# Advancing the urgent and the ordinary queue of side work beside each weight tile, and moving where sums of activations are made

## The chip, the cores and the metric

One core of one Trainium2 chip runs the kernel. The metric is the device time of one execution in microseconds. TensorE (PE) multiplies, and PEld is its weight load; VectorE (DVE), ScalarE (ACT), GpSimd (POOL) and SyncE (SP) are the other engines.

## What is computed

One hybrid block on 256 tokens of width 4096, in fp32: an RMS norm, a wide projection, an mLSTM branch with eight heads, a sparse attention branch with sixteen heads in four groups, gates on both branches, an output projection with a residual, and a gated extra embedding at the end. Cut to what matters:

```python
h = _rmsnorm(x, norm_w[layer])
u = h @ w_in[layer]
(ml_q, ml_k, ml_v, ml_o, ml_z, ml_i, ml_f, ns_q, ..., ns_g, ns_z) = _split(u, IN_SPLITS)
...
hm = _rmsnorm(_mlstm(mq, mk, mv, log_i, log_f).astype(x.dtype), ml_head_norm_w[layer])
y_ml = hm.reshape(B, S, ML_WIDTH) * jax.nn.sigmoid(ml_o) * jax.nn.silu(ml_z)
y_ns = _nsa(...) * jax.nn.silu(ns_z)
x = x + jnp.concatenate([y_ml, y_ns], axis=-1) @ w_out[layer]
x = x + jax.nn.sigmoid(x @ ple_gate[layer]) * (p[layer] @ ple_proj[layer])
```

## The kernel before

The weights are streamed once through on-chip memory in tiles of 128 by 1024, and nearly all the time goes to products of such tiles with activations. A product in fp32 is made from three: ScalarE copies a tile `raw` to `whi` in a rounded format (L1308), VectorE subtracts to get the rest `wlo` (L1309), activations are split the same way into `sh` and `sl`, and TensorE adds up `whi` with `sh`, `whi` with `sl` and `wlo` with `sh`. The activations of one pass lie in eight chunks of 512 of the 4096 features, `sh[c]` and `sl[c]`, each of two halves; a half, 256 features, is called a kp (chunk c holds kps 2c and 2c+1).

The program is one list of units in a fixed order; a unit is one weight tile and its matmuls. The main loop splits the tile three units ahead (`LOOK = 3`), emits the unit's matmuls, calls its `post`, and then calls `step()`. There are first the "wide" groups, which make the projections `kc` to `mv3` (16 units each, L816 and L818), and then 14 "pair" groups: -6 to -1 make gates from the normed input (activations `x`), 0 to 3 the output projection (activations `y`), 4 to 7 the last gate (activations `r`). Groups from 4 on start with two `p` units for the extra embedding's own projection.

In a pair group the six kps of `MIXED` (3, 5, 7, 9, 11, 13) are computed with seven block products in place of eight. For that, sums of weight blocks are made on VectorE (`raw`, L1133 to L1137) and sums of activation blocks, which are called `cb`: VectorE forms four blocks `s` from additions and subtractions, ScalarE rounds them to `cb` (high part) and VectorE subtracts for the low part. I call that a mix of a kp. A mixed step is six units: two that open it (`a_units`), two of an ordinary kp (`c_unit`), two that close it (`c_units`). `PLANS` says which kps are mixed in which group: all six in most groups, 7, 9 and 11 in group -6, and 9, 11 and 13 in group 0. The first unit of a mixed step requires the flag of its mix, which `require` gets by calling `step()` until it is there.

Where the sums of activations are made differs by pass. For `x`, `t_xmix` makes all six in the order of `MIXED`; it is queued behind the last part of the mLSTM, when the last wide group ends. For `y` and `r`, `t_stat` transposes the finished activations chunk by chunk (L723), rounds them to `sh` (L734 to L744), subtracts for `sl` (L749 to L758), makes the blocks `s` of the chunk's mixed half from a copy (L762 to L764), and then `cb` (L768, L771). It is queued twice per pass: chunks 0 and 1 when group -1 (or 3) closes its last mixed step, chunks 2 to 7 at its end.

All work beside the matmuls is written as generators that stand in two queues: `urgent` (evacuation of finished accumulators: `t_evac`, `t_mv`, `t_gate_own`, `t_x1_oth`, `t_x1_own`, `t_out_own` and others) and `fifo` (all else, in order: attention, mLSTM, mixes, `t_stat`). `step()` takes one advance from the first queue that has one:

```python
def step():
    for queue in (urgent, fifo):
        while queue:
            try:
                next(queue[0])
                return True
```

`t_gate_own` adds a finished group's accumulators to `us` (L1037), applies the activation function on ScalarE (`u`, L1045) and multiplies on VectorE (`y`, L1051). The attention of one group of heads, `t_nq`, is a pipeline over eight units (head and half of the tokens) in which step i does the scores of unit i, their bias and maximum, the exponential, and for earlier units `coef` (reciprocal and multiplication, L511 and L512), `scale` (L516), `trans` (transposes, L523), `copy_pt` (copy of the transposed probabilities, L528) and `pv`.

Of the kernel before, what the change touches and what calls it, by code (L numbers as in the profile page):

```python
# [41 lines left out]


MIXED = (3, 5, 7, 9, 11, 13)


def _plan(head, mixed, between, tail):
# [25 lines left out]
def hymba_block(ctx: ExitStack, tc: tile.TileContext, a, out: bass.AP):  # L73
# [87 lines left out]
    fifo, urgent = deque(), deque()  # L161
    done = set()

    def step():
        for queue in (urgent, fifo):
            while queue:
                try:
                    next(queue[0])
                    return True
                except StopIteration:  # L170
                    queue.popleft()
        return False
# [242 lines left out]
    def t_nq(flag, g):  # L415
# [124 lines left out]
        def at(f, i):  # L540
            if 0 <= i < 8:
                f(i)

        for i in range(11):
            at(trans, i - 2)
            at(pv, i - 3)
            at(scores, i)
            at(copy_pt, i - 2)
            at(coef, i - 1)
            at(bias_max, i)  # L550
            at(scale, i - 1)
            at(expo, i)
            yield
        if g % 2 == 0:
# [121 lines left out]

    cb = {}

    def mixed_tiles(kp):
        if kp in (3, 5):  # L680
            t = wk.tile([128, 2, 4, 128], F32R, tag="qt", name="cb", bufs=2)
        elif kp == 7:
            t = wk.tile([128, 2, 4, 128], F32R, tag="sq", name="cb")
        elif kp == 13:
            return [wk.tile([128, 4, 128], F32R, tag="pt", name="cb", bufs=2) for _ in range(2)]
        else:
            if kp == 9:
                held["cb"] = wk.tile([128, 2, 2, 4, 128], F32R, tag="b", name="cb")
            t = held["cb"][:, int(kp == 11)]
        return t[:, 0], t[:, 1]  # L690

    def t_xmix():

        f = {}
        for i in range(len(MIXED) + 1):
            if i:
                nc.vector.tensor_sub(cb[MIXED[i - 1]][1], f[i - 1], cb[MIXED[i - 1]][0])
                done.add(f"x{MIXED[i - 1] // 2}m")
            if i == len(MIXED):
                return  # L700
            c, b = MIXED[i] // 2, 2 * (MIXED[i] % 2)
            v = f[i] = stile([128, 4, 128])
            nc.vector.tensor_add(v.rearrange("p a t -> p (a t)"), sh[c][:, b:b + 2].rearrange("p k t -> p (k t)"),
                                 sl[c][:, b:b + 2].rearrange("p k t -> p (k t)"))
            nc.vector.tensor_sub(v[:, 3:0:-2], v[:, 1::-1], v[:, 3:0:-2])
            nc.vector.tensor_sub(v[:, 0], v[:, 0], v[:, 3])
            nc.vector.tensor_sub(v[:, 2], v[:, 2], v[:, 0])
            yield
            cb[MIXED[i]] = mixed_tiles(MIXED[i])
            nc.scalar.activation(cb[MIXED[i]][0], v, AF.Copy)  # L710
            yield

    def t_stat(chunks, weighted, bset=1, pace=2):


        def chunk(c, col0, gate, flag):
# [10 lines left out]
            for half in range(2):  # L727
                p, hs = pp[half], slice(2 * half, 2 * half + 2)
                w = [hnw[:, col0 // 128 + 2 * half + i:col0 // 128 + 2 * half + i + 1] for i in range(2)] if scales else None
                if 2 * c + half in MIXED:  # L730
                    f[half] = stile([128, 4, 128])
                    if scales:
                        for i in range(2):
                            nc.scalar.activation(f[half][:, 2 * i:2 * i + 2].rearrange("p a t -> p (a t)"), p[:, i],  # L734
                                                 AF.Copy, scale=w[i])
                        nc.scalar.activation(sh[c][:, hs].rearrange("p k t -> p (k t)"),
                                             f[half].rearrange("p a t -> p (a t)"), AF.Copy)
                        continue
                    nc.scalar.activation(f[half].rearrange("p a t -> p (a t)"), p.rearrange("p a t -> p (a t)"), AF.Copy)
# [21 lines left out]
            for v in f.values():  # L761
                nc.vector.tensor_sub(v[:, 3:0:-2], v[:, 1::-1], v[:, 3:0:-2])  # L762
                nc.vector.tensor_sub(v[:, 0], v[:, 0], v[:, 3])
                nc.vector.tensor_sub(v[:, 2], v[:, 2], v[:, 0])  # L764
            yield
            for half, v in f.items():
                cb[2 * c + half] = mixed_tiles(2 * c + half)
# [3 lines left out]
                nc.vector.tensor_sub(cb[2 * c + half][1], v, cb[2 * c + half][0])  # L771
            done.add(flag + "m")

        under_way, waiting, pause = deque(), deque(chunks), 0
        while under_way or waiting:
            for _ in range(len(under_way)):
                g = under_way.popleft()
# [78 lines left out]
    def p1_post(name):  # L856
# [3 lines left out]
        def post(ps, flag):  # L860
# [13 lines left out]
            elif kind in ("mq", "mk"):  # L874
                evac(ps, flag)
                add(t_mqk(flag, int(kind == "mk"), i))
                if name == "mk0":
                    add(t_mlstm(0))
            elif kind == "mv":
                if i == 2:  # L880
                    require("nq3")
                urgent.append(t_mv(ps, flag, i))
                if i == 3:
                    add(t_mlstm(1), t_xmix())
        return post

    def small_group():
# [174 lines left out]
    def pair_group(g, w, stat):  # L1062
# [39 lines left out]
        def new_activations(g, chunks, b):  # L1102

            if g < 0:
                add(t_stat([(c, (c * 512 + 2048) % 4096, f"p1_{c}", f"y{c}") for c in chunks], range(16), b))
            else:
                add(t_stat([(c, c * 512, f"p2_{c}", f"r{c}") for c in chunks], (), b))

        def finish(kp):
            if g in (-1, 3):  # L1110
# [250 lines left out]
    for n in range(N):  # L1361
# [9 lines left out]
        if un["post"]:  # L1371
            un["post"]()
        if n >= 3:
            step()
    while step():
        pass

# [82 lines left out]
```

## Time and profile before

| what | value |
|---|---|
| median of 3 runs | 2183.65 us (2182.29 to 2184.06) |
| the profiled execution's own time | 2184.17 us |
| its span in the profile | 2182.4 us |
| mean granted clock of TensorE | 0.994 |
| TensorE matmul busy | 2149.3 us, 98% |
| TensorE weight load busy | 1761.2 us, 81% |
| VectorE busy | 1563.6 us, 72% |
| ScalarE busy | 1153.8 us, 53% |
| DMA, mean over the span | 193 GB/s |

The span runs from the first to the last instruction that the profile shows; the time of the execution has 1.8 us around it. Busy shares are averages over stages. Matmuls are pipelined and overlap in the trace: a row for one of 512 columns reads 0.39 us, while in a full stretch their starts are 0.22 to 0.23 us apart. A granted clock of 1.00 is 2.4 GHz, and 0.50 is 1.2 GHz.

### The profile page before, as it was taken

What the parts mean: (1) busy time and instruction counts of PE and PEld (TensorE: products, weight loads), DVE (VectorE), ACT (ScalarE), POOL (GpSimd) and SP (SyncE); (2) the same over time, 40 slices, a digit from 0 to 9 for tenths busy, and PEclk for the clock granted to TensorE, in tenths of its full rate; (3) what the DMA queues carried; (4) which work ended last, traced back from release to release, by engine and by line L of the source; (5) the groups of instructions that cost most, each with busy time, mean ns of one, the idle gap of its engine ahead of it and who ended that gap; (6) DMA issues with size and microseconds to landing.
All of it is one profiled execution on the core that took longest, in us unless ns stands there. A gap on an engine that the chain in (4) does not pass through costs nothing.

```text
span 2182.4 us, 26787 instructions
## 1 busy us (share of the span) xinstructions
PE 2149.3 (98%) x9795; PEld 1761.2 (81%) x9795; DVE 1563.6 (72%) x1965; ACT 1153.8 (53%) x1468; POOL 32.2 (1%) x70
## 2 busy tenths in 40 slices
PE   9999999999999999998999999999999999999998
PEld 7876888787878788886888888877888887888887
DVE  6553555555555576548888888877898896888888
ACT  7543443545454555454555555555555555555554
POOL 1000000000000000000000000000000000000000
PEclk9999999999999999999999999999999999999999
DMA  9557555454544455544556566556665664556664
GB/s 379 199 195 267 189 190 181 132 187 131 188 133 168 135 195 172 192 157 164 183 201 222 186 201 218 188 188 218 206 226 183 200 227 149 203 200 222 202 217 142
DMA packets 118244, 422.08 MB, mean 193 GB/s; under 512 B 13650, under 2 KB 13962, under 8 KB 118112
## 3 DMA queue, kind: packets, MB, share of 16 engines
q1 hardware_dynamic: 114272, 409.00, 55.9%
q0 software_dynamic: 3696, 11.35, 1.6%
q8 instruction: 77, 1.26, 0.2%
q14 instruction: 55, 0.45, 0.1%
q10 hardware_dynamic: 144, 0.02, 0.0%
HBM read 416.08 MB, written 4.23 MB: 193 GB/s over the span
## 4 chain that ended last, share of the span: by engine, by line
PE 92%; DVE 4%; ACT 3%; issue 1%; DMA 0%; SPq 0%; ACTq 0%; DVEq 0%
PE mm L1059 28%; PE sd L1059 25%; PE mm L816 22%; PE mm L818 11%; DVE wlo L1309 1%; ACT whi L1308 1%; PE sd L922 1%; ACT s L506 1%; PE sd L534 1%; PE sd L237 0%; PE sd L723 0%; PE sd L523 0%; DVE mx L501 0%; PE sd L537 0%; DVE s L499 0%
## 5 line engine op out<-in xcount | busy, mean ns | idle before, releaser
L1309 DVE TENSOR_TENSOR wlo<-raw,whi 128x1024 fp32r<-128x1024 f32 x818 | 999.2, 1224 | 552.6 <-ACT whi L1308 536.8
L1308 ACT ACTIVATE whi<-raw 128x1024 fp32r<-128x1024 f32 x818 | 863.6, 1060 | 794.7 <-PE mm L816 268.4
L816 PE MATMUL mm<-whi,sh 128*128 128x512 f32 x1152 | 362.4, 396 | 0.8 <-ACT whi L1308 0.8
L816 PE MATMUL mm<-whi,sl 128*128 128x512 f32 x1152 | 355.6, 390 | 0.0
L818 PE MATMUL mm<-wlo,sh 128*128 128x512 f32 x1152 | 355.5, 390 | 0.1
L818 PEld LDWEIGHTS mm<-wlo,sh 128*128 128x128 f32 x1152 | 216.2, 188 | 46.1 <-DVE wlo L1309 0.5
L816 PEld LDWEIGHTS mm<-whi,sl 128*128 128x128 f32 x1152 | 216.3, 188 | 45.9
L1059 PE MATMUL mm<-whi,sh 128*128 128x512 f32 x740 | 241.9, 396 | 8.4 <-DVE sl L758 7.9
L816 PEld LDWEIGHTS mm<-whi,sh 128*128 128x128 f32 x1152 | 210.6, 188 | 48.8 <-issue 5.9
L1059 PE MATMUL mm<-wlo,sh 128*128 128x512 f32 x740 | 238.6, 392 | 1.7 <-DVE wlo L1309 1.6
L1059 PE MATMUL mm<-whi,sl 128*128 128x512 f32 x740 | 239.2, 393 | 0.0
L1059 PE MATMUL sd<-whi,sh 128*128 128x512 f32 x677 | 219.7, 390 | 0.0
L1059 PE MATMUL sd<-whi,sl 128*128 128x512 f32 x677 | 219.5, 389 | 0.0
L1059 PE MATMUL sd<-wlo,sh 128*128 128x512 f32 x677 | 219.4, 389 | 0.0
L1059 PEld LDWEIGHTS mm<-whi,sh 128*128 128x128 f32 x740 | 139.0, 190 | 37.9 <-issue 9.3
L1059 PEld LDWEIGHTS mm<-wlo,sh 128*128 128x128 f32 x740 | 140.0, 190 | 32.1 <-DVE wlo L1309 2.7
L1059 PEld LDWEIGHTS mm<-whi,sl 128*128 128x128 f32 x740 | 140.6, 190 | 29.4
L1059 PEld LDWEIGHTS sd<-whi,sl 128*128 128x128 f32 x677 | 127.2, 188 | 26.5
L1059 PEld LDWEIGHTS sd<-wlo,sh 128*128 128x128 f32 x677 | 127.2, 188 | 26.4
L1059 PEld LDWEIGHTS sd<-whi,sh 128*128 128x128 f32 x677 | 126.9, 188 | 26.2
L1059 PE MATMUL mm<-whi,cb 128*128 128x512 f32 x318 | 104.4, 393 | 9.6 <-ACT cb L710 8.7
L1059 PE MATMUL sd<-whi,cb 128*128 128x512 f32 x282 | 94.0, 390 | 0.0
(302 smaller groups left out, 1677.3 us busy)
## 6 DMA issues: line engine op xcount, KB each, us to landing
raw<-in_w_in SPq DMA_DIRECT2D x287, 512.0 KB, 3.5
raw<-in_w_gate SPq DMA_DIRECT2D x192, 512.0 KB, 3.6
raw<-in_w_out SPq DMA_DIRECT2D x128, 512.0 KB, 3.6
raw<-in_ple_gate SPq DMA_DIRECT2D x128, 512.0 KB, 3.5
raw<-in_w SPq DMA_DIRECT2D x16, 512.0 KB, 3.5
u<-in_xt SPq DMA_DIRECT2D x16, 256.0 KB, 7.7
xn<-in_x SPq DMA_DIRECT2D x4, 1024.0 KB, 8.9
x<-in_x POOLq DMA_DIRECT2D x4, 1024.0 KB, 9.4
```

Of the source, the lines that this page charges most:

```text
L506: nc.scalar.activation(sb[i][:, b], sb[i][:, b], AF.Exp, bias=mx[i][:, b:b + 1], accum_out=sums[i][:, b:b + 1])
L534: MM(o[t][:, h, :], ptb[i][:, b, s, :], v[:, s, b, g * 128:(g + 1) * 128], start=(b == 0 and s == 0), stop=False)
L816: MM(box["ps"][t], s[c][:, k, t * 128:(t + 1) * 128], m[:, j, :], start=st, stop=False)
L818: MM(box["ps"][t], sh[c][:, k, t * 128:(t + 1) * 128], lo[:, j, :], start=False, stop=last)
L922: MM(o[64 * kv:64 * kv + 60], xq[l // 8][:, l % 8, 60 * kv:60 * kv + 60], raw[:, j, 256 * kv:256 * kv + 256], start=(l == 0), stop=(l == 31))
L1059: MM(acc.t, s, m, start=acc.i == 0, stop=acc.i == acc.n - 1)
L1308: nc.scalar.activation(hi, r, AF.Copy)
L1309: nc.vector.tensor_sub(lo, r, hi)
```

## The change

It does four things. The main loop advances both queues beside each unit, so an urgent step no longer takes the place of an ordinary one. In the attention pipeline, `coef` and `scale` of a unit are emitted ahead of the transposes, the second product, the scores and `copy_pt`. The mixes for `x` are made in two parts: kps 7, 9, 11 queued when `mk1` ends, into another buffer, and kps 3, 5, 13 queued behind the last part of the mLSTM. In `t_stat`, chunks 1 to 3 no longer make their mixes; the three kps 3, 5, 7 are made by the same routine as for `x`, queued behind the second `t_stat`, from `sh + sl` where a copy of the accumulator was used. The first `t_stat` of a pass also waits two calls before its first chunk. Line numbers after it are higher by 1 to 7.

```diff
--- before.py
+++ after.py
@@ -42,6 +42,7 @@
 
 
 MIXED = (3, 5, 7, 9, 11, 13)
+EARLY, LATE = (3, 5, 13), (7, 9, 11)
 
 
 def _plan(head, mixed, between, tail):
@@ -161,8 +162,8 @@
     fifo, urgent = deque(), deque()
     done = set()
 
-    def step():
-        for queue in (urgent, fifo):
+    def step(queues=None):
+        for queue in queues or (urgent, fifo):
             while queue:
                 try:
                     next(queue[0])
@@ -542,13 +543,13 @@
                 f(i)
 
         for i in range(11):
+            at(coef, i - 1)
+            at(scale, i - 1)
             at(trans, i - 2)
             at(pv, i - 3)
             at(scores, i)
             at(copy_pt, i - 2)
-            at(coef, i - 1)
             at(bias_max, i)
-            at(scale, i - 1)
             at(expo, i)
             yield
         if g % 2 == 0:
@@ -676,7 +677,7 @@
 
     cb = {}
 
-    def mixed_tiles(kp):
+    def mixed_tiles(kp, tag="b"):
         if kp in (3, 5):
             t = wk.tile([128, 2, 4, 128], F32R, tag="qt", name="cb", bufs=2)
         elif kp == 7:
@@ -685,20 +686,20 @@
             return [wk.tile([128, 4, 128], F32R, tag="pt", name="cb", bufs=2) for _ in range(2)]
         else:
             if kp == 9:
-                held["cb"] = wk.tile([128, 2, 2, 4, 128], F32R, tag="b", name="cb")
+                held["cb"] = wk.tile([128, 2, 2, 4, 128], F32R, tag=tag, name="cb")
             t = held["cb"][:, int(kp == 11)]
         return t[:, 0], t[:, 1]
 
-    def t_xmix():
+    def t_mix(kps, flag, early=False):
 
         f = {}
-        for i in range(len(MIXED) + 1):
+        for i in range(len(kps) + 1):
             if i:
-                nc.vector.tensor_sub(cb[MIXED[i - 1]][1], f[i - 1], cb[MIXED[i - 1]][0])
-                done.add(f"x{MIXED[i - 1] // 2}m")
-            if i == len(MIXED):
+                nc.vector.tensor_sub(cb[kps[i - 1]][1], f[i - 1], cb[kps[i - 1]][0])
+                done.add(f"{flag}{kps[i - 1] // 2}m")
+            if i == len(kps):
                 return
-            c, b = MIXED[i] // 2, 2 * (MIXED[i] % 2)
+            c, b = kps[i] // 2, 2 * (kps[i] % 2)
             v = f[i] = stile([128, 4, 128])
             nc.vector.tensor_add(v.rearrange("p a t -> p (a t)"), sh[c][:, b:b + 2].rearrange("p k t -> p (k t)"),
                                  sl[c][:, b:b + 2].rearrange("p k t -> p (k t)"))
@@ -706,11 +707,11 @@
             nc.vector.tensor_sub(v[:, 0], v[:, 0], v[:, 3])
             nc.vector.tensor_sub(v[:, 2], v[:, 2], v[:, 0])
             yield
-            cb[MIXED[i]] = mixed_tiles(MIXED[i])
-            nc.scalar.activation(cb[MIXED[i]][0], v, AF.Copy)
-            yield
-
-    def t_stat(chunks, weighted, bset=1, pace=2):
+            cb[kps[i]] = mixed_tiles(kps[i], "a" if early else "b")
+            nc.scalar.activation(cb[kps[i]][0], v, AF.Copy)
+            yield
+
+    def t_stat(chunks, weighted, bset=1, pace=2, pause=0):
 
 
         def chunk(c, col0, gate, flag):
@@ -727,7 +728,7 @@
             for half in range(2):
                 p, hs = pp[half], slice(2 * half, 2 * half + 2)
                 w = [hnw[:, col0 // 128 + 2 * half + i:col0 // 128 + 2 * half + i + 1] for i in range(2)] if scales else None
-                if 2 * c + half in MIXED:
+                if 2 * c + half in MIXED and c >= 4:
                     f[half] = stile([128, 4, 128])
                     if scales:
                         for i in range(2):
@@ -762,6 +763,8 @@
                 nc.vector.tensor_sub(v[:, 3:0:-2], v[:, 1::-1], v[:, 3:0:-2])
                 nc.vector.tensor_sub(v[:, 0], v[:, 0], v[:, 3])
                 nc.vector.tensor_sub(v[:, 2], v[:, 2], v[:, 0])
+            if not f:
+                return
             yield
             for half, v in f.items():
                 cb[2 * c + half] = mixed_tiles(2 * c + half)
@@ -771,7 +774,7 @@
                 nc.vector.tensor_sub(cb[2 * c + half][1], v, cb[2 * c + half][0])
             done.add(flag + "m")
 
-        under_way, waiting, pause = deque(), deque(chunks), 0
+        under_way, waiting = deque(), deque(chunks)
         while under_way or waiting:
             for _ in range(len(under_way)):
                 g = under_way.popleft()
@@ -876,12 +879,14 @@
                 add(t_mqk(flag, int(kind == "mk"), i))
                 if name == "mk0":
                     add(t_mlstm(0))
+                if name == "mk1":
+                    add(t_mix(LATE, "x", True))
             elif kind == "mv":
                 if i == 2:
                     require("nq3")
                 urgent.append(t_mv(ps, flag, i))
                 if i == 3:
-                    add(t_mlstm(1), t_xmix())
+                    add(t_mlstm(1), t_mix(EARLY, "x"))
         return post
 
     def small_group():
@@ -1102,9 +1107,11 @@
         def new_activations(g, chunks, b):
 
             if g < 0:
-                add(t_stat([(c, (c * 512 + 2048) % 4096, f"p1_{c}", f"y{c}") for c in chunks], range(16), b))
+                add(t_stat([(c, (c * 512 + 2048) % 4096, f"p1_{c}", f"y{c}") for c in chunks], range(16), b, pause=2 - 2 * b))
             else:
-                add(t_stat([(c, c * 512, f"p2_{c}", f"r{c}") for c in chunks], (), b))
+                add(t_stat([(c, c * 512, f"p2_{c}", f"r{c}") for c in chunks], (), b, pause=2 - 2 * b))
+            if b:
+                add(t_mix((3, 5, 7), "y" if g < 0 else "r"))
 
         def finish(kp):
             if g in (-1, 3):
@@ -1371,7 +1378,8 @@
         if un["post"]:
             un["post"]()
         if n >= 3:
-            step()
+            step([urgent])
+            step([fifo])
     while step():
         pass
 
```

Matmuls, loads and splits keep their order; POOL and SP have the same instructions in the same order. VectorE shows the three places below. Names there: `wlo` is a weight split, `raw` a sum of weight blocks, `s` and `cb` a mix.

The start of group 0 on VectorE, before (`u<-sd_10707,u` is the last of the four additions of group -1's accumulators, `y` its products, `sl_11404` chunk 1):

```order
L1037 TENSOR_TENSOR u<-sd_10707,u 128x512
L1309 TENSOR_TENSOR wlo<-raw,whi 128x1024
L1051 SCALAR_TENSOR_TENSOR y_7303<-y_7303,rr,u 128x256 x8
L758 TENSOR_TENSOR sl_11404<-mm_11353,sh_11403 128x512
L758 TENSOR_TENSOR sl_11404<-mm_11354,sh_11403 128x512
L762 TENSOR_TENSOR s<-s 128x2x128
L763 TENSOR_TENSOR s<-s 128x128
L764 TENSOR_TENSOR s<-s 128x128
L1309 TENSOR_TENSOR wlo<-raw,whi 128x1024
L771 TENSOR_TENSOR cb<-s,cb 128x512
```

and with the change (`sl_11364` is chunk 1, `sl_11448` chunk 2):

```order
L1042 TENSOR_TENSOR u<-sd_10707,u 128x512
L759 TENSOR_TENSOR sl_11364<-mm_11335,sh_11363 128x512
L759 TENSOR_TENSOR sl_11364<-mm_11336,sh_11363 128x512
L1316 TENSOR_TENSOR wlo<-raw,whi 128x1024 x2
L1056 SCALAR_TENSOR_TENSOR y_7304<-y_7304,rr,u 128x256 x4
L1316 TENSOR_TENSOR wlo<-raw,whi 128x1024
L759 TENSOR_TENSOR sl_11448<-sd_11415,sh_11447 128x512
```

Chunk 1's `sl` moved from behind a split and the eight `y` products to directly behind the additions, and its mix is gone from there.

The opening of kp 9 in group 0 on VectorE, before (`sl_11742` is chunk 6, `sl_11804` chunk 7):

```order
L1316 TENSOR_TENSOR wlo<-raw,whi 128x512
L1309 TENSOR_TENSOR wlo<-raw,whi 128x1024
L771 TENSOR_TENSOR cb<-s,cb 128x512
L755 SCALAR_TENSOR_TENSOR sl_11804<-sd_11774,hnw_c,sh_11803 128x256 x2
L755 SCALAR_TENSOR_TENSOR sl_11804<-sd_11775,hnw_c,sh_11803 128x256 x2
L1309 TENSOR_TENSOR wlo<-raw,whi 128x1024
L1133 TENSOR_TENSOR raw<-raw 128x512
L1134 TENSOR_TENSOR raw<-raw 128x512
L1309 TENSOR_TENSOR wlo<-raw,whi 128x1024
L1136 TENSOR_TENSOR raw<-raw 128x512
```

and with the change (`sl_11746` is chunk 7; `s<-sh_11363,sl_11364` begins the mix of kp 3, `s<-sh_11447,sl_11448` that of kp 5):

```order
L774 TENSOR_TENSOR cb<-s,cb 128x512
L756 SCALAR_TENSOR_TENSOR sl_11746<-sd_11714,hnw_c,sh_11745 128x256 x2
L756 SCALAR_TENSOR_TENSOR sl_11746<-sd_11715,hnw_c,sh_11745 128x256 x2
L1323 TENSOR_TENSOR wlo<-raw,whi 128x512
L704 TENSOR_TENSOR s<-sh_11363,sl_11364 128x512
L706 TENSOR_TENSOR s<-s 128x2x128
L707 TENSOR_TENSOR s<-s 128x128
L708 TENSOR_TENSOR s<-s 128x128
L1316 TENSOR_TENSOR wlo<-raw,whi 128x1024 x2
L1140 TENSOR_TENSOR raw<-raw 128x512
L1141 TENSOR_TENSOR raw<-raw 128x512
L698 TENSOR_TENSOR cb<-s,cb 128x512
```

Chunk 7 and the mix of chunk 6 moved ahead of the opening by two splits, and the mixes of kps 3, 5 and 7 now lie among its first splits and weight sums.

One step of attention on VectorE, before (`pt` is the copy of transposed probabilities, `sm_3928` the reciprocal and its multiplication):

```order
L1309 TENSOR_TENSOR wlo<-raw,whi 128x1024
L528 COPY pt<-sd_3949 128x256
L511 RECIPROCAL sm_3928<-sm_3928 128x2
L512 TENSOR_TENSOR sm_3928<-sm_3928,sg 128x2
L499 TENSOR_TENSOR s<-sd_3952,tb 128x256
L501 TENSOR_REDUCE mx_3964<-s 128x2
```

and with the change:

```order
L1316 TENSOR_TENSOR wlo<-raw,whi 128x1024
L512 RECIPROCAL sm_3910<-sm_3910 128x2
L513 TENSOR_TENSOR sm_3910<-sm_3910,sg 128x2
L529 COPY pt<-sd_3935 128x256
L500 TENSOR_TENSOR s<-sd_3938,tb 128x256
L502 TENSOR_REDUCE mx_3948<-s 128x2
```

The copy moved behind the reciprocal and the multiplication on which the scaling waits.

## Rows read from the trace of the kernel before

**Rows 1.** The page's first table: busy us (share of the span) and instructions per engine.

```profile
PE 2149.3 (98%) x9795; PEld 1761.2 (81%) x9795; DVE 1563.6 (72%) x1965; ACT 1153.8 (53%) x1468; POOL 32.2 (1%) x70
```

**Rows 2.** Windows: length, then busy us (instructions) per engine, TensorE's granted clock, DMA share, GB/s.

```profile
990.00:995.00 5.00, 0.16 (x1) 0.16 (x1) 3.44 (x9) 1.26 (x2) 0.00 (x0) 0.50 0.04 16
1460.00:1465.00 5.00, 2.59 (x6) 1.95 (x7) 3.78 (x10) 2.62 (x6) 0.00 (x0) 0.53 0.14 57
1515.00:1520.00 5.00, 3.29 (x14) 2.16 (x13) 4.96 (x10) 0.95 (x2) 0.00 (x0) 1.00 0.57 212
1530.00:1580.00 50.00, 50.00 (x222) 41.35 (x221) 42.54 (x49) 25.73 (x27) 0.00 (x0) 1.00 0.63 206
```

**Rows 3.** Waits of TensorE: line and releaser, total us, times, longest us.

```profile
PE mm L1059 <- ACT cb L710: 8.7, 1, 8.7
PE mm L1059 <- DVE sl L758: 7.9, 2, 5.4
PE sd L523 <- ACT s L516: 1.9, 4, 0.8
PE mm L1059 <- DVE wlo L1309: 1.6, 1, 1.6
PE mm L1059 <- ACT whi L1308: 0.9, 1, 0.9
```

**Rows 4.** Timeline, opening of kp 7 in group -6: start, us, instruction, idle before and releaser.

```profile
994.84 0.79 PE L1059 MATMUL mm<-whi,cb 128*128 128x512 f32 x1 [8.68 <-ACT cb L710]
1000.32 0.62 PE L1059 MATMUL mm<-whi,sl 128*128 128x512 f32 x2
...
988.63 0.69 DVE L697 TENSOR_TENSOR cb<-s,cb 128x512 fp32r<-128x512 f32 x1
989.23 0.68 DVE L703 TENSOR_TENSOR s<-sh,sl 128x512 f32<-128x512 f32 x1
991.72 0.69 DVE L697 TENSOR_TENSOR cb<-s,cb 128x512 fp32r<-128x512 f32 x1 [0.69 <-ACT cb L710]
...
991.06 0.63 ACT L710 ACTIVATE cb<-s 128x512 fp32r<-128x512 f32 x1 [4.93 <-DVE s L707]
```

**Rows 5.** Timeline, start of group 0, on TensorE, VectorE and ScalarE.

```profile
1462.41 1.36 PE L1059 MATMUL mm<-whi,sh 128*128 128x512 f32 x2 [5.36 <-DVE sl L758]
1467.52 0.63 PE L1059 MATMUL mm<-whi,sh 128*128 128x512 f32 x2
...
1454.14 2.65 DVE L1037 TENSOR_TENSOR u<-sd,u 128x512 f32<-128x512 f32 x4 [0.17 <-PE sd L1059]
1458.40 3.25 DVE L1051 SCALAR_TENSOR_TENSOR y<-y,rr,u 128x256 f32<-128x256 f32 x8 [0.48 <-ACT u L1045]
1461.58 1.28 DVE L758 TENSOR_TENSOR sl<-mm,sh 128x512 fp32r<-128x512 f32 x2
...
1456.35 1.28 ACT L1045 ACT_TABLE_LOAD   x1
1457.65 2.56 ACT L1045 ACTIVATE u<-u,rt 128x512 f32<-128x512 f32 x4
```

**Rows 6.** Timeline, start of group 4, on TensorE.

```profile
1811.18 1.25 PE L1059 MATMUL mm<-whi,sh 128*128 128x512 f32 x2 [2.58 <-DVE sl L758]
1815.49 0.63 PE L1059 MATMUL mm<-wlo,sh 128*128 128x512 f32 x2
```

**Rows 7.** Timeline, ScalarE's mixes of two successive chunks before kp 9 of group 0.

```profile
1502.94 0.63 ACT L768 ACTIVATE cb<-s 128x512 fp32r<-128x512 f32 x1 [3.44 <-DVE s L764]
1511.03 0.63 ACT L768 ACTIVATE cb<-s 128x512 fp32r<-128x512 f32 x1 [3.87 <-DVE s L764]
```

**Rows 8.** Attention: idle time before its transposes, a copy, VectorE's part of an evacuation.

```profile
  ACT s L516: 12.2, 32
...
434.22 0.42 DVE L528 COPY pt<-sd 128x256 f32<-128x256 f32 x1
...
L188 DVE TENSOR_SCALAR u<-mm,rt 128x512 f32<-128x512 f32 x5 | 3.7, 749 | 2.6 <-PE mm L818 2.6
```

## The prediction

> **What bounds the kernel now.** I read the busy table first: TensorE is busy 2149.3 us, 98% of the span [rows 1]. A window in full swing shows what that means: 222 matmuls of 512 columns in 50 us at granted clock 1.00, 0.225 us each, with VectorE busy for 42.54 of the 50 [rows 2]. Such stretches can't be made shorter by moving side work; what can go is time in which TensorE doesn't keep that pace. Two windows beside it show such places: 0.16 us of work in 5 us, and six matmuls in 5 us at clock 0.53 [rows 2]. The table of TensorE's waits then names them: 8.7 us on `cb` once, 7.9 us on `sl` in two waits, 1.6 on `wlo` and 0.9 on `whi` [rows 3]. I went to each in the timeline.
>
> Place A is the opening of mixed step kp 7 in group -6. TensorE is idle for 8.68 us before 994.84, waiting for ScalarE's `cb`; from there it needs 5.48 us (to 1000.32) for 14 matmuls that take 3.15 at pace [rows 4]. That extra 2.33 us is the clock: the granted clock reads 0.50 in the window of the wait [rows 2], which is the lower level, 1.2 GHz. A costs 8.68 + 2.33 = 11.0 us. Its cause stands in the same rows: VectorE makes mixes of kps 3, 5, 7 one after the other, because the opening needs kp 7 and the queue hands out kp 3 and 5 first. From one `cb` subtraction (988.63) to the next (991.72) is 3.09 us, 0.69 of it idle, so one mix holds VectorE for 2.40 us; ScalarE sat 4.93 us idle before its `cb` copy [rows 4].
>
> Place B1 is the first unit of group 0: idle 5.36 us on `sl` at 1462.41, then 12 matmuls in 5.11 us (to 1467.52) for 2.70, together 7.8 us [rows 5]. VectorE's `sl` for chunk 1 starts only at 1461.58, since ScalarE first did a table load (1456.35) and four `u` (1457.65, 2.56) before chunk 1's `sh`, and VectorE the eight `y` products (1458.40, 3.25) [rows 5].
>
> Place C is the same in group 4: idle 2.58 us at 1811.18, then 10 matmuls in 4.31 (to 1815.49) for 2.25, together 4.6 us [rows 6]. Place B2 is the opening of kp 9 in group 0: the 1.6 on `wlo` and 0.9 on `whi` [rows 3], 2.5 us. There ScalarE's `cb` for successive chunks comes at 1502.94 and 1511.03, 8.09 us apart, each time after an idle wait on VectorE's `s` [rows 7]. In attention the 32 groups of transposes found their `s` late by 12.2 us in all [rows 8], most of it in the weight-load queue, where it partly lies beside matmuls still running. The four places make 25.9 us; attention's true part I put at 5, between the 1.9 of TensorE's own wait for it [rows 3] and 12.2.
>
> **The change part by part.**
>
> *Mixes for the first pass.* Kps 7, 9, 11 are now made while the `mv` units run, and kps 3, 5, 13 one per two units from the opening on. The 8.68 us wait was on kp 7 behind kps 3 and 5, so it goes, and with it the 2.33 us at low clock. What is late next: three mixes, 3 x 2.40 = 7.2 us of VectorE, fall in six units, which are one mixed step: 45 matmuls, 10.1 us of TensorE. By the 50 us row VectorE has 7.46 free in 50 [rows 2], so 1.5 in 10.1; 5.7 us are over. Weight tiles are split three units ahead, and the three in front of the opening have 12 matmuls each, 8.1 us of TensorE; that covers the 5.7 if the lookahead is full. I take 0.7 us of loss, nearer the covered end; the ends are 0 and 5.7 + 2.33 = 8.0. Gain **10.3** (3.0 to 11.0).
>
> *Start of group 0.* The pause of 2 and a fifo step beside each urgent step make both chunks' transposes one unit earlier, so that `sh` of chunk 1 stands ahead of the table load, and `sl` of chunk 1 directly behind the `own` additions, ahead of two weight splits and the `y`. The additions start at 1454.14 and take 2.65 [rows 5]; one `sl` pair takes 1.28 [rows 5], so it is done at about 1458.1, while TensorE runs out of work 5.36 us before 1462.41, at 1457.0. That is a wait of 1.1 us; a weight split now queued behind `sl` adds to it, and I take 1.6. A wait that long on `wlo` [rows 3] left the granted clock at 1.00 in its window, 1515 to 1520 [rows 2], so I add nothing for the clock. Ends: 0, and 7.8 if the wait only changes its name. Gain **6.2**. The table load holds ScalarE from 1456.35 to the next instruction at 1457.65, 1.30 us [rows 5]. The Trainium skill ("ScalarE: Activation LUTs", What ACT_TABLE_LOAD costs) gives about 1283 ns for the load and another 1380 ns of drain at each switch of set; the row shows the first and hardly any of the second. Were the drain paid here, the weight copies now queued behind the load would come up to 1.36 us later, and the sum below would be an estimated 18.6 in place of 20.0; the trace speaks against it.
>
> *Start of group 4.* The same, without a table load. The wait there was shorter, and I leave 1.4 of 4.6 (ends 0 and 4.6). Gain **3.2**.
>
> *Opening of kp 9, group 0.* Chunks 1 to 3 no longer make mixes there, and chunks 4 to 7 come one chunk slot earlier, so the 2.5 us could vanish. But kps 3, 5, 7 of the next group are now made behind chunk 7, in the very units that open kp 9: 7.2 us of VectorE, with ScalarE's `cb` copies in line ahead of weight copies. Ends: 0, and 7.2 + 2.4 for a fall of the clock as at B1, 9.6. Because TensorE reaches this place with more tiles in hand than now, I take 3.1. Gain **-0.6** (-7.1 to 2.5). In group 4 the same three mixes stand beside two more ordinary units; I take 0.3 (ends 0 and 4). Gain **-0.3**.
>
> *Attention.* The reciprocal, its multiplication and the scaling now stand ahead of the copy of transposed probabilities on VectorE. That copy is 0.42 us at the smaller size [rows 8], so the scaling starts some 0.3 to 0.6 us sooner, about the 12.2 / 32 = 0.38 us by which a transpose was late. I count 3.2 of the 5 us as gained. Against it, an evacuation now shares a unit with an attention step: 0.75 us of VectorE [rows 8] and about as much of ScalarE, in four heads' groups; I take 0.5 for each, 2.0. Gain **1.2**; ends -6 (four times 0.75 on either engine, one behind the other) and 5.
>
> The ACT copy that three chunks per set drop (six in all) and the `s` addition that takes its place are inside the 2.40 us of a mix. Loads and their order are unchanged, as are POOL and SP.
>
> Sum: 10.3 + 6.2 + 3.2 - 0.6 - 0.3 + 1.2 = **20.0 us**. The profiled execution took 2184.17 us (span 2182.4), so 2164.2; the median of the runs is 0.52 lower, so **2163.6**.
>
> **Rivals.**
>
> *(a) More goes.* The openings lose nothing at kp 9 and attention gains 3.5: 10.3 + 6.2 + 3.2 + 2.5 + 3.5 = 25.7, time 2157.9. For it: VectorE has spare time in every steady window. Against it: the mixes land in the busiest units. Chance 0.25.
>
> *(b) VectorE falls behind at the openings.* The displaced mixes cost 3 at A, 8 at kp 9 of group 0 with a clock fall, 4 in group 4, the rest as forecast: 8.0 + 6.2 + 3.2 - 5.5 - 4.0 + 1.2 = 9.1, time 2174.5. For it: the present ring of 8.09 us between `cb` copies [rows 7]. Against it: the lookahead of three tiles. Chance 0.18.
>
> *(c) Slower.* One mechanism, ScalarE's weight copy blocked behind a `cb` copy that waits on VectorE: if each of the three openings (kp 7 of group -6, kp 9 of groups 0 and 4) stalls as A does now, 3 x 11.0 = 33.0, with 3.0 left at the group starts, 36.0 against 25.9: 10.1 us more, less attention's 1.2, time 2192.5. It decides from (25.9 + 1.2 - 3.0) / 3 = 8.0 us per opening on. Against it: A's stall was a series of three mixes demanded at once, and no opening demands that now. Chance 0.03.
>
> *(d) Nothing measurable.* The waits change names: the group starts wait on the `own` additions and the openings on the splits, for as long. Time about 2183.6. Chance 0.04.
>
> **How the numbers follow.** The forecast has 0.50, and the others stand above. A measurement of this kernel can tell about 0.2%, 4.4 us. Faster by more: forecast, (a) and (b), 0.93; within: (d), 0.04; slower: (c), 0.03. The range takes in (a) with attention's better end, and most of (b): 2155 to 2173.
>
> **What would show it.** In the changed profile the 8.7 us wait on `cb` must be gone from TensorE's waits, and the window 990 to 995 at full pace. The waits on `sl` should be two of under 2 us, with no window at half clock at either group start. Waits on `wlo` or `whi` at the opening of kp 9 of group 0 should be about 3 us. The transposes' lateness on `s` should fall from 12.2 us to some 5. The forecast is wrong if a new wait over 2 us with a fallen clock stands at an opening (then b or c), or if the two `sl` waits keep their length (then d).

## The result and the profile after

The changed kernel takes 2169.69 us (median of 4 runs, 2169.23 to 2169.96) against 2183.61 before: a ratio of 0.9937, 95% interval 0.9920 to 0.9954. It is faster by 13.9 us where 20.0 were forecast, and inside the range given. The profiled execution has a span of 2168.1 us for 2182.4, 14.3 less, and a mean granted clock of 0.999.

The page's busy table hardly shows it; the row that answers to [rows 1] is

```profile
PE 2146.1 (99%) x9795; PEld 1756.3 (81%) x9795; DVE 1565.5 (72%) x1971; ACT 1152.1 (53%) x1462; POOL 32.1 (1%) x70
```

TensorE's share went from 98% to 99%. The Trainium skill says that matmul busy time is a poor measure of how near a kernel is to its limit ("Perfetto Trace Analysis", Identifying the Most-Contended Engine); these two pages of the profile agree: the half-clock stretches that went had counted as busy, as in the window at 1460, where TensorE is busy 2.59 us at clock 0.53 [rows 2].

TensorE's waits, to be read against [rows 3] (line, releaser, total us, times, longest):

```profile
PE sd L524 <- ACT s L517: 4.2, 9, 0.6
...
PE mm L1064 <- DVE sl L759: 1.9, 2, 1.0
PE mm L1064 <- DVE wlo L1316: 1.9, 3, 1.6
PE sd L1064 <- DVE wlo L1316: 1.7, 2, 1.5
PE sd L524 <- DVE s L500: 1.0, 2, 0.6
```

The 8.7 us on `cb` are gone, the two waits on `sl` fell from 7.9 to 1.9 in all, and the waits on `wlo` are longer (3.6 in five, for 1.6). The transposes' wait on `s` grew from 1.9 to 4.2, and a wait on VectorE's `s` (the bias addition, by that kernel's line L500) is new.

**Where the time went.** The 8703 matmuls on weight tiles come in the same order in every kernel here. So the start of the k-th can be compared, and the time between two of them is a stage. For each kernel the table gives how much more (+) or less (-) time it takes for a stage than the kernel before, in us, from the starts in one profiled execution each. The boundaries are given in the time of the kernel before, and lie where every kernel has run the same number of TensorE's other matmuls; a boundary that some of those have crossed would book them as a gain on one side and a loss on the other.

| kernel | start, to 328 us | wide groups with attention and mLSTM, up to kp 7, to 981 | opening of kp 7 (A), to 1020 | groups -6 to -1, to 1417 | start of group 0 and opening of kp 9 (B1, B2), to 1549 | start of group 4 (C), 1776 to 1902 |
|---|---|---|---|---|---|---|
| forecast |  | -1.2 | -10.3 |  | -5.6 | -2.9 |
| changed | -0.3 | +4.0 | -10.5 | +1.0 | -5.6 | -2.9 |
| e1_step_attn | -1.0 | -1.8 | -10.5 | +1.0 | -5.5 | -3.0 |
| e2_old_order | +0.1 | +5.8 | -10.5 | +1.0 | -5.6 | -3.0 |
| e3_both | -0.3 | -0.1 | -10.5 | +1.0 | -5.6 | -3.0 |
| e4_spread | -0.5 | +3.9 | -10.5 | +1.0 | -8.4 | -1.7 |
| e5_best | -0.6 | -1.9 | -10.5 | +1.0 | -8.4 | -3.0 |
| e6_empty_unit | -1.2 | -2.7 | -10.5 | +1.0 | -5.6 | -3.0 |
| e7_one_mix | -0.6 | +4.0 | -0.9 | 0.0 | -5.8 | -3.0 |
| e8_chunk_mix | -0.7 | +4.0 | -10.5 | +1.0 | -6.3 | -3.2 |
| e9_two_empty | +0.1 | -6.6 | -10.5 | +1.0 | -8.4 | -3.0 |
| e10_one_step | -1.1 | -1.8 | -8.9 | +1.0 | +1.7 | -2.6 |
| e11_step_only | -0.7 | +5.7 | -1.0 | 0.0 | -7.8 | +0.7 |
| e12_no_pause | -1.4 | -6.7 | -10.5 | +1.0 | -7.2 | +0.9 |

Stages that are left out differ by 0.0. The changed kernel's row adds up to -14.3. Against the forecast's row, which adds up to -20.0, nearly all of the shortfall of 5.7 stands in one column: attention was to gain 1.2 and lost 4.0. (The expectations below say 4.6. They go by a boundary at 944, where four mLSTM matmuls, 0.7 us, stand on the other side, and their gain of 1.7 at the opening of kp 7 is too large by the same.) The first column varies without an edit as well: e9 and e12 are the same up to there and differ by 1.5.

The windows at the three repaired places (columns as in [rows 2]):

```profile
996.00:1001.00 5.00, 4.82 (x21) 3.67 (x20) 4.81 (x9) 3.06 (x5) 0.00 (x0) 1.00 0.54 141
1450.00:1455.00 5.00, 3.91 (x21) 2.85 (x20) 3.87 (x7) 4.33 (x6) 0.00 (x0) 1.00 0.32 107
1797.00:1802.00 5.00, 3.91 (x20) 2.77 (x19) 4.13 (x7) 1.75 (x2) 0.00 (x0) 1.00 0.37 105
```

No clock is below 1.00 where [rows 2] showed 0.50 and 0.53. At the start of group 0 the rows that answer to [rows 5] are

```profile
1452.25 1.06 PE L1064 MATMUL mm<-whi,sh 128*128 128x512 f32 x2 [0.96 <-DVE sl L759]
...
1449.03 2.48 DVE L1042 TENSOR_TENSOR u<-sd,u 128x512 f32<-128x512 f32 x4
1451.42 1.28 DVE L759 TENSOR_TENSOR sl<-mm,sh 128x512 fp32r<-128x512 f32 x2
...
1449.51 1.06 ACT L1315 ACTIVATE whi<-raw 128x1024 fp32r<-128x1024 f32 x1 [1.66 <-PE sd L1064]
1450.59 1.28 ACT L1050 ACT_TABLE_LOAD   x1
1451.89 1.34 ACT L1050 ACTIVATE u<-u,rt 128x512 f32<-128x512 f32 x2
```

VectorE's `sl` now follows the additions directly, and TensorE waits 0.96 us for it. Group 4 starts with the same wait of 0.96. The copy ahead of the table load ends at 1450.57, the load stands at 1450.59 and the next ScalarE instruction at 1451.89: 1.30 us again, with 0.02 ahead of it. The drain of 1380 ns that the Trainium skill adds ("ScalarE: Activation LUTs", What ACT_TABLE_LOAD costs) does not show here either, and the sum by the skill's price falls.

### The profile page after: what moved, and what is told of

The parts are those of the page before. It is cut to its first block, busy times and chain, and to the rows that moved or that the text cites. A ratio compares the mean times of both kernels' runs of the same rounds, so it can differ in the third digit from the quotient of the medians.

```text
span 2168.1 us, 26804 instructions
## 1 busy us (share of the span) xinstructions
PE 2146.1 (99%) x9795; PEld 1756.3 (81%) x9795; DVE 1565.5 (72%) x1971; ACT 1152.1 (53%) x1462; POOL 32.1 (1%) x70
```

## Experiments

In the sets of runs the kernel before reads 2183.1 to 2184.0 us, so where two kernels differ by about 1 us the table of stages is needed beside the times.

### Attention: the doubled step or the new order

The transposes' lateness rose from 12.2 us in 32 cases [rows 8] to

```profile
  ACT s L517: 19.1, 41
```

Two theories: the doubled step costs it (T1), or the new order does (T2). Three kernels part them. `e1_step_attn`:

```diff
-            step([urgent])
-            step([fifo])
+            if "nq3" in done:
+                step([urgent])
+                step([fifo])
+            else:
+                step()
```

> The changed kernel gained 13.9 us where 20.0 were forecast; aligned matmul by matmul, its attention stage lost about 4.6 us where 1.2 were to be gained. This kernel takes one step per unit, urgent before ordinary, until the last attention group is done, and both after that; the new order inside attention stays. Theory T1 (the doubled step removed the unit without attention work in which VectorE and ScalarE caught up, and put an evacuation into an attention unit): the loss goes, 2164 to 2166. Theory T2 (the new order of coef and scale costs it): nothing changes, 2169.7. If the forecast's gain from the order is right as well, it is at 2163 or below.

Measured 2163.43 us (2163.28 to 2164.07), just below the range of T1. `e2_old_order` keeps the doubled step and puts the old order back:

```diff
-            at(coef, i - 1)
-            at(scale, i - 1)
             at(trans, i - 2)
             at(pv, i - 3)
             at(scores, i)
             at(copy_pt, i - 2)
+            at(coef, i - 1)
             at(bias_max, i)
+            at(scale, i - 1)
             at(expo, i)
```

> The changed kernel with the old order inside attention (transposes, second product, scores, copy, then coef and scale). T1: no gain, 2169.7 to 2173, the upper end if the new order is worth the 3.2 us of the forecast. T2: about 4.6 us less, 2165.

Measured 2171.50 us (2170.83 to 2171.95). `e3_both` has both edits.

> Both undone for the attention stage, so it is the attention stage of before with all later parts of the change. Either theory: about 2165, the changed kernel less 4.6. Its distance to e1_step_attn is the worth of the new order alone: 3 us by the forecast, 0 if the wait of the transposes is set by something else.

Measured 2165.64 us (2165.53 to 2165.99). T2 falls: the new order gains, 2171.50 - 2169.69 = 1.8 us beside the doubled step and 2165.64 - 2163.43 = 2.2 without it. The doubled step in attention costs 2169.69 - 2163.43 = 6.3 us with the new order and 5.9 with the old; the table has 5.8 and 5.9.

What in it costs? `e6_empty_unit` leaves the doubled step and only adds one empty advance per attention group, so that one unit has no attention step; evacuations still fall into attention units:

```diff
             at(expo, i)
             yield
+            if i == 2:
+                yield
```

> The changed kernel with one empty advance in each attention group, between its first and second transposes; evacuations still share units with attention. It parts T1 in two. T1a (what was lost is the unit in which the other engines caught up): most comes back, at least 0.6 us at each of four groups, 2165 to 2167.5. T1b (the evacuation beside an attention step is what costs): 2169 to 2170.

Measured 2162.68 us (2162.21 to 2163.34), 7.0 less than the changed kernel and below the whole range given for T1a. VectorE's order shows that the evacuation (`mv`) still stands in an attention step, right ahead of its reciprocal and the product:

```profile
403.76 0.75 DVE L189 TENSOR_SCALAR mv<-mm,rt 128x512 f32<-128x512 f32 x1
404.42 0.16 DVE L512 RECIPROCAL sm<-sm 128x2 f32<-128x2 f32 x1
404.61 0.16 DVE L513 TENSOR_TENSOR sm<-sm,sg 128x2 f32<-128x2 f32 x1
```

So beside an empty unit, an evacuation in an attention unit costs nothing that shows; what was lost is a unit without attention. By the starts of the matmuls the gain over the changed kernel stands in the four attention groups, 1.6 to 1.9 us in each, and does not change between them. (e1_step_attn gets less, since in the last attention group no evacuation takes a unit.) The lateness of the transposes, 19.1 us in the changed kernel, is now

```profile
  ACT s L517: 7.9, 24
```

The rows suggest why one unit is worth so much. In the changed kernel, late in an attention group and beside an evacuation (starts of transposes on TensorE, then VectorE, ScalarE):

```profile
420.85 0.84 PE L524 MATMUL sd<-idn,s 128*128 128x128 f32 x4
...
431.01 0.84 PE L524 MATMUL sd<-idn,s 128*128 128x128 f32 x4 [0.36 <-ACT s L517]
...
521.01 0.84 PE L524 MATMUL sd<-idn,s 128*128 128x128 f32 x4 [0.58 <-DVE s L500]
...
519.34 0.74 DVE L189 TENSOR_SCALAR mv<-mm,rt 128x512 f32<-128x512 f32 x1
520.00 0.15 DVE L512 RECIPROCAL sm<-sm 128x2 f32<-128x2 f32 x1
...
520.45 0.91 ACT L517 ACTIVATE s<-s,sm 128x256 f32<-128x256 f32 x2 [1.71 <-DVE sm L513]
```

Two units, with 49 matmuls on TensorE, take 431.01 - 420.85 = 10.16 us, and beside an evacuation the transposes at 521.01 come no sooner than the scaling at 520.45 allows, which waited 1.71 us for VectorE's `sm`, behind `mv` at 519.34 (the profile names the bias addition, the last VectorE instruction before, as releaser). In e9_two_empty below, where nothing is late, the same 49 matmuls take 9.45:

```profile
424.94 0.60 PE L524 MATMUL sd<-idn,s 128*128 128x128 f32 x4
...
434.39 0.60 PE L524 MATMUL sd<-idn,s 128*128 128x128 f32 x4
```

A pair of attention units thus loses up to 0.71 us as soon as the other engines' lead is used up. That TensorE's own work does not set the pace there shows in the two units before, from 410.75 to 420.85: they hold 52 matmuls, three more, and take 10.10. Before the change the urgent evacuation had a unit to itself, without an attention step. In the kernel before, the transposes on either side of it are

```profile
399.09 0.38 PE L523 MATMUL sd<-idn,s 128*128 128x128 f32 x2
...
405.12 0.60 PE L523 MATMUL sd<-idn,s 128*128 128x128 f32 x4
```

which is 6.03 us apart with two units' weight matmuls between them; in the changed kernel it is 3.91 (396.08 and 399.99) with one. In the extra unit TensorE had 12 weight matmuls, 2.7 us, and the other engines a split and the evacuation, so they could get ahead again. The doubled step took that unit away. That the lead of the other engines is what the unit restores is my reading of these rows; shown is that the unit is worth 7.0 us. Which of the links (weight copy, split, exponential, scaling) sets the 10.16 was not taken apart.

### The mixes at the opening of kp 9

In the changed kernel TensorE waits twice for `wlo` there, and VectorE is in the mixes meanwhile:

```profile
1507.68 0.73 PE L1064 MATMUL mm<-wlo,sh 128*128 128x512 f32 x2 [1.57 <-DVE wlo L1316]
...
1513.59 0.50 PE L1064 MATMUL sd<-wlo,cb 128*128 128x512 f32 x1 [1.54 <-DVE wlo L1316]
...
1504.69 0.68 DVE L704 TENSOR_TENSOR s<-sh,sl 128x512 f32<-128x512 f32 x1
...
1506.40 1.22 DVE L1316 TENSOR_TENSOR wlo<-raw,whi 128x1024 fp32r<-128x1024 f32 x1
```

`e4_spread` begins the three mixes five units later and five units apart:

```diff
-    def t_mix(kps, flag, early=False):
+    def t_mix(kps, flag, early=False, gap=0):
...
             if i == len(kps):
                 return
+            for _ in range(gap):
+                yield
...
-                add(t_mix((3, 5, 7), "y" if g < 0 else "r"))
+                add(t_mix((3, 5, 7), "y" if g < 0 else "r", gap=5))
```

> The changed kernel with the mixes of kps 3, 5 and 7 for y and r begun five units later and five units apart, instead of one after the other at the opening of kp 9. The forecast's reason for the opening (three mixes of 2.40 us pile up on VectorE there): the 3.8 us lost there and about 1 us at the opening in group 4 go, 2165 to 2166. Rival (the chunks' own ring through ScalarE and VectorE costs it, as in the kernel before): 2169 to 2170.

Measured 2168.10 us (2167.49 to 2168.32), between the two values expected. The opening of kp 9 in group 0 gains 2.8 us (-8.4 for -5.6 in the table) of the 3.8 expected, in the direction that the pile-up predicts. Group 4 loses 1.2 in place of a gain: I take it that the two `p` units had hidden the mixes there and that, spread out, they meet full units, but this was not tested. `e5_best` spreads for y alone, with e1's step:

```diff
-                add(t_mix((3, 5, 7), "y" if g < 0 else "r"))
+                add(t_mix((3, 5, 7), "y" if g < 0 else "r", gap=5 if g < 0 else 0))
```

> One step per unit until attention is done, as in e1_step_attn, and the mixes of kps 3, 5, 7 spread as in e4_spread, but for y alone (there e4 gained about 3.0 us; for r, where two units without mixes stand ahead, spreading lost 1.2). If the two places are independent: 2163.4 less 3.0, 2160.4 (2159.5 to 2161.5). Rival, the lookahead lost at one place comes back at the next: 2162 to 2163.

Measured 2161.04 us (2160.76 to 2161.51): inside the first range, 2.4 less than e1.

`e8_chunk_mix` makes these mixes inside chunks 1 to 3 again:

```diff
-                if 2 * c + half in MIXED and c >= 4:
+                if 2 * c + half in MIXED:
...
-            if b:
-                add(t_mix((3, 5, 7), "y" if g < 0 else "r"))
```

> The changed kernel with the mixes of kps 3, 5, 7 made inside chunks 1 to 3 of t_stat again, as before. If the group starts improved because chunk 1's sl moved ahead of the table load and the products (doubled step and pause), they keep their gain and the opening of kp 9 loses about as much as now (3 to 4 us): 2169 to 2171. Rival, taking the mixes out of the chunks is what helped the starts: the waits on sl return in part, 2172 to 2177.

Measured 2168.57 us (2168.48 to 2168.67), 1.1 less than the changed kernel and just below the range. The group starts keep their gain without this part of the change, so the rival falls. Where the change put the mixes is slightly worse than where they were.

### The mixes for x

`e7_one_mix` makes all six in one series again, with the doubled step:

```diff
-                if name == "mk1":
-                    add(t_mix(LATE, "x", True))
...
-                    add(t_mlstm(1), t_mix(EARLY, "x"))
+                    add(t_mlstm(1), t_mix(MIXED, "x"))
```

> The changed kernel with all six mixes for x in one series in the old order 3, 5, 7, 9, 11, 13 behind the last part of the mLSTM. By the forecast's reading of place A (kp 7 waits behind kps 3 and 5): a stall on cb returns at the opening of kp 7; since the doubled step lets the series start some units earlier, fewer mixes are left for that moment, and 3 to 7 us return, 2172.5 to 2177. Rival, the doubled step alone removed the stall: 2169.5 to 2171. Full return: 2181.

Measured 2178.13 us (2177.70 to 2178.29): 8.4 us return, more than the 3 to 7 expected and less than the 11 of a full return. TensorE's wait, and the windows after 992:

```profile
PE mm L1062 <- ACT cb L711: 7.6, 1, 7.6
```

and

```profile
992.00:997.00 5.00, 0.00 (x0) 0.00 (x0) 4.35 (x8) 0.85 (x2) 0.00 (x0) 0.57 0.31 105
997.00:1002.00 5.00, 4.79 (x11) 3.76 (x12) 3.07 (x6) 2.53 (x4) 0.00 (x0) 0.50 0.00 0
```

The stall is back with 1.2 GHz behind it. The doubled step alone is worth 0.9 of the 10.5 us of this stage; the earlier kps 7, 9, 11 are worth 9.6.

### The step and the pause at the group starts

`e10_one_step` takes one step per unit throughout:

```diff
-            step([urgent])
-            step([fifo])
+            step()
```

> The changed kernel with one step per unit throughout. Attention gains 6.3 as in e1_step_attn. If the doubled step is what moved chunk 1's sl ahead of the table load and the products, both group starts stall again, by 7.8 or more and 4.6 or more: 2172 to 2176. Rival, the pause and the later mixes alone keep the group starts short: 2163 to 2165.

Measured 2172.74 us (2172.08 to 2173.09). The wait at the start of group 0 is back:

```profile
PE mm L1064 <- DVE sl L759: 7.5, 2, 5.8
```

One of the two is 5.8 us long: `sl` starts at 1450.01, behind the eight `y` products at 1446.84. But the start of group 4 keeps 2.6 of its 2.9 us, against what I expected: there the pause and the later mixes suffice, and only at group 0, with a table load and products ahead of chunk 1, is the doubled step needed. That the time lies in the range is partly luck: the stall that did not come in group 4 is in part made up by 1.6 us lost at the opening of kp 7 (-8.9 for -10.5), where TensorE waits 0.74 us for `wlo` and 0.51 for `whi`.

`e11_step_only` is the kernel before with the doubled step and nothing else:

```diff
-    def step():
-        for queue in (urgent, fifo):
+    def step(queues=None):
+        for queue in queues or (urgent, fifo):
...
-            step()
+            step([urgent])
+            step([fifo])
```

> The kernel before with the doubled step alone. Attention loses 4.6 plus the 1.8 that the new order is worth beside it (e2_old_order), 6.4; the opening of kp 7 stalls as in e7_one_mix, 1.7 better than before; the two waits on sl go, 7.8 and 4.6, since chunk 1's sl then stands even ahead of the own additions: 2183.7 + 6.4 - 1.7 - 12.4, about 2176 (2174 to 2178). Rival, without the pause chunk 1 waits for something else and the starts stall: 2183 or more.

Measured 2182.12 us (2179.24 to 2184.09, a wide spread), ratio 0.9993 with interval 0.9984 to 1.0003: no change that can be told, and my sum was 6 us off. The rival's mechanism, a wait for something else, is what came. The waits of TensorE say where:

```profile
PE mm L1059 <- ACT cb L710: 7.6, 1, 7.6
PE sd L523 <- ACT s L516: 6.7, 11, 0.8
PE mm L723 <- DVE s L959: 3.3, 1, 3.3
```

The stall at kp 7 and the attention loss are there, 4.7 together as summed, but in place of the waits on `sl` come new ones at L723: the transposes of chunks 0 and 1 stand so early in TensorE's order that they wait for VectorE to finish the previous accumulators (`s` at L959 here, `u` at the start of group 0, 1.7 and 1.4 us), and all matmuls behind them wait too. The stage of group 0 still gains 7.8, that of group 4 loses 0.7.

`e9_two_empty` joins what was learnt: the doubled step throughout, two empty advances per attention group, and e5's spread for y:

```diff
             at(expo, i)
             yield
+            if i in (2, 6):
+                yield
```

> The changed kernel with two empty advances in each attention group (behind its steps 2 and 6), and the mixes of kps 3, 5, 7 for y spread as in e5_best. In e6_empty_unit one advance left two small losses per group, together about 0.9 us at three of four groups. If a catch-up unit is what counts, the second takes most of that away: 2162.7 less 2.4 (e5 against e1) less 2.0, about 2158.3 (2157.5 to 2159.5). Rival, the later work pushed back by eight units collides at the opening of kp 7: 2160 or more.

Measured 2156.11 us (2156.00 to 2156.85), ratio to before 0.9876, interval 0.9861 to 0.9891: the fastest kernel here, 13.6 us below the changed one and 2.2 below what I expected. What TensorE still waits for:

```profile
PE sd L124 <- ACT u L121: 2.7, 1, 2.7
PE mm L1068 <- DVE sl L763: 1.9, 2, 1.0
PE mm L1068 <- DVE wlo L1320: 0.5, 2, 0.4
PE mm L1068 <- ACT mv L187: 0.3, 1, 0.3
PE sd L1068 <- DVE wlo L1320: 0.2, 1, 0.2
```

No wait for attention is left in this view. `e12_no_pause` takes the pause out of it:

```diff
-                add(t_stat([...], range(16), b, pause=2 - 2 * b))
+                add(t_stat([...], range(16), b))
...
-                add(t_stat([...], (), b, pause=2 - 2 * b))
+                add(t_stat([...], (), b))
```

> As e9_two_empty, without the pause of two calls in the first t_stat of a pass. Chunk 1's sl then stands ahead of the own additions of the finished group. If the 1.5 us still lost at each group start come from those additions: 3 us less than e9, about 2155.3. Rival, the earlier chunk runs into the last mixed step of the group, where VectorE is full: no gain, or 1 to 2 us lost.

Measured 2162.42 us (2160.43 to 2163.29): 6.3 us slower, the rival, and by more than it allowed. The timeline at the end of group 3, on TensorE and VectorE, and a window after it:

```profile
1769.03 1.25 PE L728 MATMUL mm<-idn,x 128*128 128x128 f32 x8 [3.27 <-DVE s L968]
1770.04 0.94 PE L1068 MATMUL sd<-whi,sh 128*128 128x512 f32 x2
...
1768.29 0.68 DVE L968 TENSOR_TENSOR s<-mm,s 128x512 f32<-128x512 f32 x1
```

and

```profile
1770.00:1774.00 4.00, 4.00 (x13) 3.17 (x12) 0.00 (x0) 0.92 (x2) 0.00 (x0) 0.57 0.43 166
```

The eight transposes wait 3.27 us for VectorE's `s` at L968, a subtraction on the finished `oth` accumulators, and the clock reads 0.57 in the 4 us from 1770. With the pause, in e9_two_empty, this wait is not there. The profiled execution is the fastest of the four, 3.6 us behind that of e9_two_empty; by the table it loses 1.2 at group 0 and 3.9 at group 4. The other three have a mean clock of 0.997 or 0.998 for its 0.999, and no trace shows where they lost the rest of the 6.3.

## Why the prediction was right, and where it was off

**Opening of kp 7.** Forecast a gain of 10.3, measured 10.5: the wait on `cb` is gone with its half-clock stretch, and the 0.7 us set aside for late splits shows as two waits of under 0.2. The cause holds by e7: with the old series the stall returns.

**Start of group 0 and opening of kp 9.** Forecast 6.2 - 0.6 = 5.6, measured 5.6, and parted between the two places 6.3 gained and 0.7 lost. The wait on `sl` is 0.96 us, near the 1.1 worked out from the additions' end and below the 1.6 taken. At the opening two waits of 1.57 and 1.54 make 3.1, the value taken. That it fits so well is in part luck: the prediction chose it between ends of 0 and 9.6, and its reason, that TensorE reaches this place with more tiles in hand, was not tested. e10 and e11 confirm that the doubled step moved chunk 1 there, e4 that the pile of mixes costs most of the 3.1 (2.8 came back). What I did not see is what the pause is for: I counted it with the step as making the transposes earlier, and e12 shows that it holds them back, behind work on which TensorE would stall.

**Start of group 4.** Forecast 3.2 - 0.3 = 2.9, measured 2.9 (3.2 gained at the start, 0.25 lost behind it).

**Attention.** This is the step that failed: a gain of 1.2 was forecast, and the loss was 4.0; the lateness of the transposes, which was to fall to some 5 us, rose to 19.1. The order's part was of the right sign, 1.8 to 2.2 us where I counted 3.2. The mis-sized term is the evacuation that now shares a unit, put at 2.0 from the length of its instructions; the doubled step in attention measured 5.9 to 6.3. With these, 2.2 - 6.3 = -4.1, the loss is accounted for. I priced what was added to a unit and overlooked what was taken: the unit in which nothing of attention ran. e6 puts it back alone and gets 7.0 us. The 5 us that the prediction gave as attention's true part were too few as well: in e9 this stage is 6.6 us shorter than before.

**Groups -6 to -1** lose 1.0 us that the forecast has no term for. It comes in steps of about 0.2 at each group, in every kernel whose opening of kp 7 doesn't stall and in none where it does (e7, e11). TensorE has no wait over 0.02 us there; single matmuls start 0.007 to 0.015 us later behind their neighbour than in the kernel before. Why is open.

Of the rivals, (b) comes nearest in time (2174.5), but not by its mechanism: no opening lost more than 0.1 us beyond the forecast. The prediction says that its range, 2155 to 2173, takes in most of (b); (b)'s own time lies outside it.

## What to carry to other kernels

A unit that seems wasted, because the side queue does something small in it, may be the one in which the other engines regain their lead; before packing side work closer, compare the pace of the packed stretch with TensorE's own. When a side step is moved earlier, look at what its first TensorE instruction waits for, since everything behind it in that engine's order waits as well. A series that is demanded at one moment is best split by who needs which part first.

## What the runs showed that I had not expected

One empty advance per attention group, four in all, is worth 7.0 us, more than the waits on `sl` and `wlo` that remain in the changed kernel (1.9 and 3.6). And in the profiled execution of e12_no_pause two idle waits close together, 1.68 and 1.42 us at the end of group -1 (timeline, then the window after it), left the clock at 1.00, while the 3.27 us at the end of group 3 were followed by 0.57 (the window shown above):

```profile
1421.81 0.66 PE L728 MATMUL mm<-idn,y 128*128 128x128 f32 x4 [1.68 <-DVE u L997]
1423.89 0.66 PE L728 MATMUL mm<-idn,y 128*128 128x128 f32 x4 [1.42 <-DVE u L999]
...
1425.00:1430.00 5.00, 5.00 (x25) 4.07 (x24) 2.02 (x3) 1.64 (x3) 0.00 (x0) 1.00 0.25 94
```

The kernel before lost TensorE's full pace behind waits of 2.58, 5.36 and 8.68 us [rows 4 to 6].
